# A hybrid trunk layer in float32: FFN down by the seven-product scheme, its block sums made early, stage joints rewritten

## Chip, cores and metric

The kernel runs on one core of a Trainium2 chip. The metric is the device time of one execution in microseconds (us). A figure for a kernel is the median of its runs.

## What is computed

One layer over 2048 tokens of width 1024, all in float32: an RMS norm, a mixing stage of two head groups (a gated MLP over chunks and a matrix-memory recurrence), an FFN with a causal depthwise convolution of three taps, a gate that adds an embedding `p`, and a last RMS norm. In short form (`W` stands for the weights):

```
h  = rms(x) ;  x1 = x + concat(gmlp(h W_uv), mlstm(h W_qkvo)) W_out
f  = rms(x1) W_up            # 2048 x 5632, two halves a, b of 2816
act = silu(conv3(a)) * conv3(b)
x2 = x1 + act W_down         # 2048 x 2816 times 2816 x 1024
out = rms(x2 + sigmoid(rms(x2) W_pg) * (p W_pe))
```

## The kernel before

**Numbers.** A float32 product is made of three matmuls on operands split in a rounded high part and a low rest: high by high, high by low, low by high. The split is a copy (ScalarE, or VectorE in `wsplit`) for the high part and a subtraction on VectorE for the low one (`wsplit` L102 for the mix stage, `halves` L678 and `split` L684 for the later ones).

**Mix stage (0 to 871 us).** Four blocks `b` of 512 tokens, one after the other. Each has four `tok_group`s (token-major products; L325 to L327), of which group 3 comes last, then eight `qk_tile`s and four `u_tile`s (L118 to L121), whose results pass a convolution on VectorE (`cv`, L480) and a SiLU on ScalarE (`qk`, L482); `head_a` (L490 to L492) is the first that needs a `qk`. Tiles 0 and 4 feed the first `head_a`. A block's residual goes to DRAM (`x1s`). The FFN's input of a block is made one block later by `make_h` (L640), called through `pend[1]()` at L439: for each of four `kk` it loads 512 KB of `x1s` into an `xs` buffer of `xpool`, scales it on VectorE (`ffn_in`, L204) and writes it to DRAM (`td`). In an odd block it also loads two 256 KB tiles (`hs`) and makes four block sums for the up product (L214, L216, L218, L220), each written out. `xpool` has two buffers, shared by `xs` and `hs`, so a `kk` can load only when the writes of the one before have landed.

**FFN (871 to 2218 us).** Two halves of 1024 tokens, each up and then down. Up multiplies 2x2 blocks by seven products in place of eight, with the order in `ORDER`; `build_t` loads the token operands from `td` into 28 slots `k`, and the block sums of `w_up` are made on the fly (`Up.prep`). Its results pass `Up.conv` and are written as `act`. Down (class `Down`, L819) is the plain product: per half two token blocks `th`, 22 steps `j`, 8 column tiles `d` and 3 matmuls, into four pairs of PSUM banks:

```
for d in range(KD):
    PE.matmul(ps, hi[:, c], t[:, :HALF], ...)     # L848
    PE.matmul(ps, hi[:, c], t[:, HALF:], ...)     # L849
    PE.matmul(ps, lo[:, c], t[:, :HALF], ...)     # L850
```

`load` brings 512 KB of `w_down` and 256 KB of `act` per step, `prep` splits both.

**Embedding stage (2218 to 2479 us).** `Ple.run` for four token blocks; the last one in two halves. The norm's chain `st1`, `st2`, `st3` of `SumSq` (L146 to L187) ends in a broadcast row `rB`.

**What sets the order.** In the FFN a table of steps (`Steps`): each step names the steps ahead at which its loads and splits are emitted. Everywhere the tile scheduler then orders each engine's list, and each engine, and SyncE (SP) which issues all the DMAs, runs its list strictly in that order, waiting at the first instruction that is not ready.

Of the kernel before, what the change touches and what calls it, by code (L numbers as in the profile page):

```python
# [15 lines left out]
P = 128  # L16
# [14 lines left out]
SLOTS = {"k": (28, 1024), "r": (7, 1024), "f": (4, 1024), "w": (2, 3072), "m": (8, 512), "x": (8, 512)}  # L31
# [10 lines left out]
def trunk_kernel(ctx: ExitStack, tc: tile.TileContext, xT, pT, w_u, w_qk, w_v0, w_v1,  # L42
# [33 lines left out]
    tds = [{q: dram.tile([P, 4, TB], F32, name=f"td{s}_{q}") for q in range(1, 8)} for s in range(NH)]  # L76
    acts = [[dram.tile([P, TH], F32, name=f"act{s}_{j}") for j in range(NJ)] for s in range(NH)]

    col = const.tile([P, NCOL], F32, name="col")
    DMA.dma_start(col, cols)  # L80

# [20 lines left out]
    def wsplit(src, n, eng=None, leng=None):  # L102
        st = wpool.tile([P, 1024], F32, tag="wst", name="wst")
        DMA.dma_start(st[:, :n], src)
# [27 lines left out]
    class SumSq:  # L132
# [48 lines left out]

        def st3(self):
# [39 lines left out]

    with mx:
        big = mx.enter_context(tc.tile_pool(name="mbig", bufs=1))
# [12 lines left out]
        for k0, k1 in ((0, 1), (1, 2), (2, 4), (4, 6), (6, 8)):  # L237
# [5 lines left out]
            if k0 == 0:  # L243
                w_first = wsplit(w_v0[0], 2 * GW[0], V, V)
# [54 lines left out]
        for b in range(NB):  # L299
# [347 lines left out]
    with ExitStack() as fx:  # L647
# [25 lines left out]
        def load2(src, nm):  # L673
            t = slot("x", nm)
            DMA.dma_start(t, src)
            return t
# [38 lines left out]

        def build_t(s, prod, kk):
            T[prod, kk] = halves(load2(tds[s][prod][:, kk, :], "hx"), "k", "tt")


        class Up:  # L720
# [66 lines left out]
            def post(self, prod):  # L787
# [14 lines left out]
                else:  # L802
                    f = self.conv(1, ub)
                    V.tensor_tensor(f, f, self.fa, ALU.mult)
                    DMA.dma_start(acts[self.s][self.j], f)

        def up_half(s, extra):
            for j in range(NJ):
                o = Up(s, j)
# [9 lines left out]
        n3 = [SumSq(Slots("m"), None, None, V) for b in range(NB)]  # L819

        class Down:
            def __init__(self, s, th):
                self.s, self.th, self.b, self.w, self.op = s, th, 2 * s + th, {}, {}

            def load(self, j):
                w = self.w[j] = slot("w", "wd")
                DMA.dma_start(w[:, 0:1024], w_down[j])
                DMA.dma_start(w[:, 1024:1536], acts[self.s][j][:, self.th * HALF:(self.th + 1) * HALF])

            def prep(self, j):  # L830
                w = self.w.pop(j)
                t = halves(w[:, 1024:1536], "r", "at")
                self.op[j] = split(w[:, 0:1024], "r", "wd") + (t,)

            def fetch(self):
                self.x = []
                for q in range(4):
                    x = pairs(slot("f", "xr"))
                    DMA.dma_start(x, x1s[self.b][:, 2 * q:2 * q + 2, :])
                    self.x.append(x)  # L840

            def mm(self, j):
                if j == 0:
                    self.ps = [bank2("dn") for _ in range(4)]
                hi, lo, t = self.op.pop(j)
                for d in range(KD):
                    ps, c = self.ps[d // 2][:, d % 2, :], slice(d * 128, (d + 1) * 128)
# [4 lines left out]
            def post(self):  # L852
                n = n3[self.b]
                for q in range(4):
# [3 lines left out]
                    for i in range(2):  # L858
                        n.add(x[:, i, :])
# [20 lines left out]
        class Ple:  # L880
# [27 lines left out]
            def out_tile(self, d, si, ps):  # L908
# [14 lines left out]
                if d == KD - 1:  # L923
                    f.st1()
# [168 lines left out]
```

## Time and profile before

| | |
|---|---|
| Runs shown | 2482.81 us median of 3 (2481.03 to 2486.6) |
| Profiled execution, its own time | 2480.78 us |
| Span in its profile | 2479.0 us |
| TensorE (PE) busy | 2404.0 us, 97% |
| VectorE (DVE) busy | 1697.2 us, 68% |
| ScalarE (ACT) busy | 1066.4 us, 43% |
| DMA | 324.99 MB, mean 131 GB/s |
| Mean granted TensorE clock | 0.990 of full speed |

A row of the profile names the line, the engine, the operation, the tile written and those read, and how many there were. A busy figure on PE counts overlapping matmuls, so the rate of a dense stretch is read from a window: its length over its number of matmuls. The bracket at the end of a timeline row gives the idle time of the engine ahead of the instruction, and what ended it.

### The profile page before, as it was taken

Reading aid. Unit: us, or ns where it says so; the run is one execution under the profiler, and the core shown is the slowest. Engines: PE = TensorE matmul, PEld = TensorE weight load, DVE = VectorE, ACT = ScalarE, POOL = GpSimd, SP = SyncE. Lnnn points to the kernel's source line nnn. Section 1 sums busy time; section 2 is a strip of 40 time slices with the busy share of each in tenths; the row PEclk is TensorE's granted clock in tenths of the full one; section 3 lists DMA queues with packets and bytes.
Section 4 is the critical chain, followed back from the end, with each engine's and each line's share of the span. In section 5 each row is a group of like instructions: output and inputs, shape, how many; then the busy total and the mean of one; then the engine's idle time right before and its main releaser. Section 6 shows DMA issues by size and latency. Waiting matters only on the chain.

```text
span 2479.0 us, 30740 instructions
## 1 busy us (share of the span) xinstructions
PE 2404.0 (97%) x11596; PEld 2039.9 (82%) x11596; DVE 1697.2 (68%) x2846; ACT 1066.4 (43%) x1707; POOL 53.5 (2%) x62
## 2 busy tenths in 40 slices
PE   8999999999999979999999999999999999989997
PEld 8888987988898858888888887788888888868887
DVE  7687667688656578888776343878877746354666
ACT  3453364256236355444455332444444435332223
POOL 1000000000000000000000000000000000000000
PEclk9999999999999989999999999999999999999999
DMA  6326424472542262344227474322222266550221
GB/s 200 96 69 213 153 85 135 151 241 70 175 132 86 94 238 77 112 157 157 94 91 258 140 250 136 120 77 77 86 93 77 97 212 206 184 189 13 68 69 68
DMA packets 125173, 324.99 MB, mean 131 GB/s; under 512 B 13664, under 2 KB 15840, under 8 KB 125024
## 3 DMA queue, kind: packets, MB, share of 16 engines
q1 hardware_dynamic: 125024, 323.02, 39.3%
q8 instruction: 91, 1.49, 0.2%
q14 instruction: 58, 0.48, 0.1%
HBM read 260.05 MB, written 62.91 MB: 130 GB/s over the span
## 4 chain that ended last, share of the span: by engine, by line
PE 89%; DVE 5%; DMA 3%; ACT 2%; issue 1%; POOL 1%; SPq 0%; DVEq 0%; POOLq 0%; ACTq 0%
PE ub L764 6%; PE ub L763 6%; PE ub L762 6%; PE dn L848 6%; PE dn L849 6%; PE dn L850 6%; PE ua L764 5%; PE ua L762 5%; PE ua L763 5%; PE acc L118 4%; PE acc L119 4%; PE acc L121 4%; PE bank L118 3%; PE bank L119 3%; PE bank L121 3%; PE acc L326 3%
## 5 line engine op out<-in xcount | busy, mean ns | idle before, releaser
L762 PE MATMUL ub<-tt,sw 128*128 128x512 f32 x704 | 276.1, 392 | 13.2 <-ACT tt L680 11.6
L848 PE MATMUL dn<-at,wd 128*128 128x512 f32 x704 | 274.1, 390 | 5.0 <-ACT wd L686 3.3
L763 PE MATMUL ub<-tt,sw 128*128 128x512 f32 x704 | 275.7, 392 | 1.3 <-DVE tt L681 1.3
L764 PE MATMUL ub<-tt,sw 128*128 128x512 f32 x704 | 275.4, 391 | 0.5 <-DVE sw L687 0.5
L849 PE MATMUL dn<-at,wd 128*128 128x512 f32 x704 | 273.9, 389 | 0.0
L850 PE MATMUL dn<-at,wd 128*128 128x512 f32 x704 | 272.5, 389 | 0.0
L686 ACT ACTIVATE sw<-wr 128x1024 fp32r<-128x1024 f32 x132 | 140.3, 1063 | 289.2 <-PE ua L763 257.6
L687 DVE TENSOR_TENSOR wd<-wd 128x1024 fp32r<-128x1024 f32 x88 | 107.9, 1226 | 198.4 <-ACT wd L686 195.1
L687 DVE TENSOR_TENSOR sw<-wr,sw 128x1024 fp32r<-128x1024 f32 x132 | 161.4, 1223 | 75.7 <-ACT sw L686 75.6
L762 PE MATMUL ua<-tt,sw 128*128 128x512 f32 x528 | 205.7, 390 | 0.7 <-ACT sn L768 0.7
L763 PE MATMUL ua<-tt,sw 128*128 128x512 f32 x528 | 205.5, 389 | 0.0
L764 PE MATMUL ua<-tt,sw 128*128 128x512 f32 x528 | 205.4, 389 | 0.0
L111 DVE TENSOR_TENSOR wlo<-wst,whi 128x1024 fp32r<-128x1024 f32 (+2 forms) x144 | 158.6, 1105 | 52.5 <-ACT whi L107 31.2
L326 PE MATMUL acc<-wlo,hh 128*128 128x384 f32 (+1 forms) x512 | 175.6, 343 | 7.8 <-DVE wlo L111 7.8
L325 PE MATMUL acc<-whi,hh 128*128 128x384 f32 (+1 forms) x512 | 172.6, 342 | 8.2 <-DVE whi L109 7.7
L686 ACT ACTIVATE wd<-wd 128x1024 fp32r<-128x1024 f32 x88 | 93.2, 1059 | 192.5 <-PE dn L849 187.4
L327 PE MATMUL acc<-whi,hl 128*128 128x384 f32 (+1 forms) x512 | 174.7, 341 | 0.0
L762 PEld LDWEIGHTS ub<-tt,sw 128*128 128x128 f32 x704 | 133.1, 189 | 42.6 <-ACT tt L680 12.7
L848 PEld LDWEIGHTS dn<-at,wd 128*128 128x128 f32 x704 | 132.1, 188 | 34.5 <-ACT wd L686 4.5
L763 PEld LDWEIGHTS ub<-tt,sw 128*128 128x128 f32 x704 | 133.1, 189 | 30.2 <-DVE tt L681 2.4
L764 PEld LDWEIGHTS ub<-tt,sw 128*128 128x128 f32 x704 | 133.1, 189 | 28.3 <-DVE sw L687 0.9
L850 PEld LDWEIGHTS dn<-at,wd 128*128 128x128 f32 x704 | 132.2, 188 | 27.8 <-DVE wd L687 0.2
(296 smaller groups left out, 5073.9 us busy)
## 6 DMA issues: line engine op xcount, KB each, us to landing
wd<-w_down SPq DMA_DIRECT2D x88, 512.0 KB, 3.6
wr<-w_up SPq DMA_DIRECT2D x44, 512.0 KB, 3.6
wr<-w_up SPq DMA_DIRECT2D x88, 256.0 KB, 4.4
act<-fc SPq DMA_DIRECT2D x44, 512.0 KB, 4.0
wd<-act SPq DMA_DIRECT2D x88, 256.0 KB, 3.9
wst<-w_v SPq DMA_DIRECT2D x48, 384.0 KB, 3.2
wst<-w_qk SPq DMA_DIRECT2D x32, 512.0 KB, 3.6
wst<-w_out SPq DMA_DIRECT2D x32, 512.0 KB, 3.5
```

Of the source, the lines that this page charges most:

```text
L118: PE.matmul(ps, wh, mh, start=(i == 0), stop=False)
L119: PE.matmul(ps, wh, ml, start=False, stop=False)
L326: PE.matmul(ps[t][:, :n], a_h, rl, start=False, stop=False)
L327: PE.matmul(ps[t][:, :n], a_l, rh, start=False, stop=(k == KD - 1))
L686: A.activation(hi, x, AF.Copy)
L687: V.tensor_tensor(lo, x, hi.bitcast(F32), ALU.subtract)
L762: PE.matmul(ps, hi[:, c], t[:, :HALF], start=first, stop=False, skip_group_check=on)
L763: PE.matmul(ps, hi[:, c], t[:, HALF:], start=False, stop=False, skip_group_check=on)
L764: PE.matmul(ps, lo[:, c], t[:, :HALF], start=False, stop=last, skip_group_check=on)
L848: PE.matmul(ps, hi[:, c], t[:, :HALF], start=(j == 0), stop=False)
L849: PE.matmul(ps, hi[:, c], t[:, HALF:], start=False, stop=False)
L850: PE.matmul(ps, lo[:, c], t[:, :HALF], start=False, stop=(j == NJ - 1))
```

## The change

1. **Down in seven products.** `Down` is now one object per half. Each of the seven products of `ORDER` has 11 steps `k` of 12 matmuls (L920 to L922 of the changed file). A step loads two tiles of 256 KB into one `x` slot (four slots of 1024 columns, before eight of 512), four steps ahead, and splits them two steps ahead (`halves`, L728 and L729). Products accumulate in two pairs of banks; between products ScalarE copies a pair aside (`snap`) or VectorE adds it to the residual (`give`).
2. **Block sums of `w_down`**: new `down_sums` for each of the 11 `k`, three in each of the blocks 0 to 2 and two in block 3, placed behind group 3: two loads of 512 KB into `xpool`, four subtractions or additions of 128x512 on VectorE, four writes of 256 KB to `sds`.
3. **Block sums of `act`**: `Up.sums` in each odd `j` of up: four such operations, four writes to `ads`.
4. **`make_h`** is called behind group 3 and behind `down_sums`, no longer ahead of group 3.
5. **Joints.** The first weight tile is loaded through ScalarE's DMA queue at the start. `build_t` loads two `kk` by one DMA of 512 KB. The norm of block 0 of the last stage (`st2b`, `st3`) moves into up of half 1. `out_tile` keeps gate and product in one pair of banks. The norm of the last two halves uses a shorter chain (`q1`, `q2`), and their output leaves in DMAs of two tiles, all from VectorE.

```diff
+    def down_sums(k, pair, one):
+        p, q = pair(), pair()
+        for i, t in enumerate((p, q)):
+            DMA.dma_start(t, w_down[2 * k + i].rearrange("p (i t) -> p i t", t=TB))
+        s5, s6, s7, s3 = one(), one(), one(), one()
+        V.tensor_tensor(s5, p[:, 1, :], q[:, 1, :], ALU.add)
+        V.tensor_tensor(s6, s5, p[:, 0, :], ALU.subtract)
+        V.tensor_tensor(s7, p[:, 0, :], p[:, 1, :], ALU.subtract)
+        V.tensor_tensor(s3, q[:, 0, :], s6, ALU.subtract)
+        for n, t in ((5, s5), (6, s6), (7, s7), (3, s3)):
+            DMA.dma_start(sds[n][:, k, :], t)
...
-            if b:
-                pend[1]()
             ps = tok_group(3)
             for t in range(CPB):
                 evac(osig[:, t, 128:512], ps[t][:, 0:384], t)
+            for k in range(3 * b, min(3 * b + 3, NJ // 2)):
+                down_sums(k, lambda: xpool.tile([P, 2, TB], F32, tag="xs", name="ds"), lambda: tt("dsum"))
+            if b:
+                pend[1]()
...
+                    self.act = pairs(f)
+                    if self.j % 2:
+                        self.sums()
...
+            def load(self, prod, k):
...
+                x = self.raw[prod, k] = pairs(slot("x", "sx"))
+                DMA.dma_start(x[:, 0, :], sw())
+                DMA.dma_start(x[:, 1, :], tm())
+
+            def prep(self, prod, k):
+                x = self.raw.pop((prod, k))
+                self.op[prod, k] = halves(x[:, 0, :], "r", "dw"), halves(x[:, 1, :], "r", "dt")
...
+                for d in range(4):
+                    ps, c = bank[d // 2][:, d % 2, :], slice(d * 128, (d + 1) * 128)
+                    first = k == 0 and prod in (1, 2, 5)
+                    last, on = k == NK - 1, prod in (6, 7, 3, 4)
+                    PE.matmul(ps, w[:, c], t[:, :HALF], start=first, stop=False, skip_group_check=on)
+                    PE.matmul(ps, w[:, c], t[:, HALF:], start=False, stop=False, skip_group_check=on)
+                    PE.matmul(ps, w[:, HALF + d * 128:HALF + (d + 1) * 128], t[:, :HALF], start=False, stop=last, skip_group_check=on)
...
         def down_half(s, extra):
+            o = Down(s)
+            for i, prod in enumerate(ORDER):
+                for k in range(NK):
+                    early = [(4, lambda prod=prod, k=k: o.load(prod, k)), (2, lambda prod=prod, k=k: o.prep(prod, k))]
...
+        at(3, 5, n3[0].st2b)
+        at(3, 3, n3[0].st3)
         up_half(1, ex)
...
-        n3[0].st2b()
-        n3[0].st3()
```

**VectorE in block 2, before.** The list ends `make_h` (L204 scales, L214 to L220 sum) with the low parts of the next weight tiles (L111) between its `kk`; the convolutions of tiles 0 and 4 (L480) follow. These are the third and the fourth `kk`.

```order
L214 TENSOR_TENSOR hx<-xs 128x512
L216 TENSOR_TENSOR hx<-xs,hs 128x512
L218 TENSOR_TENSOR hx<-hx,hs 128x512
L220 TENSOR_TENSOR hx<-hs,hx 128x512
L111 TENSOR_TENSOR wlo<-wst,whi 128x1024 x2
L204 SCALAR_TENSOR_TENSOR xs<-xs,col,rB 128x512 x2
L214 TENSOR_TENSOR hx<-xs 128x512
L216 TENSOR_TENSOR hx<-xs,hs 128x512
L218 TENSOR_TENSOR hx<-hx,hs 128x512
L220 TENSOR_TENSOR hx<-hs,hx 128x512
L111 TENSOR_TENSOR wlo<-wst,whi 128x1024
L480 SCALAR_TENSOR_TENSOR cv<-ub,col,cv 128x512 x6
```

The first two `kk` stood further up, ahead of group 3's last weights and behind them.

**VectorE in block 2, changed.** First the place from group 3's last copy (`osig`) to the first `kk`: the rest of the second `down_sums` and the whole third one (L256 to L259), weights of the tiles (L117, the old L111), then the first scaling (L231, the old L204).

```order
L373 TENSOR_SCALAR osig<-acc 128x384
L257 TENSOR_TENSOR dsum<-dsum,ds 128x512
L258 TENSOR_TENSOR dsum<-ds 128x512
L259 TENSOR_TENSOR dsum<-ds,dsum 128x512
L117 TENSOR_TENSOR wlo<-wst,whi 128x1024 x2
L256 TENSOR_TENSOR dsum<-ds 128x512
L257 TENSOR_TENSOR dsum<-dsum,ds 128x512
L258 TENSOR_TENSOR dsum<-ds 128x512
L259 TENSOR_TENSOR dsum<-ds,dsum 128x512
L117 TENSOR_TENSOR wlo<-wst,whi 128x1024 x2
L231 SCALAR_TENSOR_TENSOR xs<-xs,col,rB 128x512 x2
```

Then the end of the same stretch: the third and the fourth `kk` (L241 to L247 are the old L214 to L220), and the convolutions of tiles 0 and 4 (L521, the old L480).

```order
L231 SCALAR_TENSOR_TENSOR xs<-xs,col,rB 128x512 x2
L241 TENSOR_TENSOR hx<-xs 128x512
L243 TENSOR_TENSOR hx<-xs,hs 128x512
L245 TENSOR_TENSOR hx<-hx,hs 128x512
L247 TENSOR_TENSOR hx<-hs,hx 128x512
L231 SCALAR_TENSOR_TENSOR xs<-xs,col,rB 128x512 x2
L241 TENSOR_TENSOR hx<-xs 128x512
L243 TENSOR_TENSOR hx<-xs,hs 128x512
L245 TENSOR_TENSOR hx<-hx,hs 128x512
L247 TENSOR_TENSOR hx<-hs,hx 128x512
L521 SCALAR_TENSOR_TENSOR cv<-ub,col,cv 128x512 x6
```

All four `kk` now stand behind the third `down_sums`, one after the other, with one weight tile between the first and the second, and the first convolution of the block stands behind the last of them. On PE the order at this place was four tiles, 16 small matmuls of `mix` (L555), two of tile 5's matmuls, `head_a`; it is now four tiles, `mix`, 18 of tile 5's matmuls, `head_a`. In blocks 1 and 3, where `make_h` makes no sums, the convolutions stand ahead of it, or behind its last scaling with the loads begun earlier.

**SP from up to down, half 0, before.** L827 and L828 load a step of down, L675 the token operands of the next half, L839 the residual; L805 writes the last `act`.

```order
L827 DMA wd<-w_down 128x1024
L828 DMA wd<-act_3_103 128x512
L839 DMA xr<-x1s_78 128x1024 x2
L675 DMA hx<-td_7_99 128x512
L675 DMA hx<-td_3_95 128x512 x2
L805 DMA act_21_121<-fc 128x1024
L839 DMA xr<-x1s_78 128x1024
L827 DMA wd<-w_down 128x1024
L828 DMA wd<-act_4_104 128x512
```

**SP at the same place, changed.** L903 and L904 load a step of down, L858 writes `act`, L872 a block sum of `act`.

```order
L903 DMA sx<-w_down 128x512
L904 DMA sx<-act_6_121 128x512
L912 DMA xr<-x1s_82 128x2048
L858 DMA act_20_135<-fc 128x1024
L872 DMA ad_5_108<-two 128x512
L858 DMA act_21_136<-fc 128x1024
L872 DMA ad_7_110<-two 128x512
L872 DMA ad_6_109<-two 128x512
L872 DMA ad_4_107<-two 128x512
L903 DMA sx<-w_down 128x512
L904 DMA sx<-act_8_123 128x512
```

Before, the loads of four steps stand ahead of the last `act` write and the fifth right behind it. Now the first four steps are loaded ahead, and the fifth stands behind the write of the last `act` and the three last block sums made from it. From up to down in half 1 the order is the same, with one more load between.

## Rows read from the trace of the kernel before

**Rows 1.** Windows, up 0 to down 1: length, busy us, clock, DMA share, GB/s.

```profile
905.00:1311.00 406.00, 405.31 (x1787) 335.06 (x1786) 342.05 (x379) 203.33 (x281) 1.01 (x1) 1.00 0.36 124
...
1433.00:1537.00 104.00, 104.00 (x459) 85.53 (x457) 42.53 (x50) 34.01 (x44) 0.00 (x0) 1.00 0.60 203
...
1565.00:1977.00 412.00, 411.54 (x1815) 340.59 (x1815) 322.68 (x430) 184.61 (x216) 2.99 (x2) 1.00 0.25 83
...
1977.00:2218.00 241.00, 241.00 (x1064) 199.42 (x1064) 115.51 (x129) 94.78 (x117) 0.00 (x0) 1.00 0.56 187
```

**Rows 2.** What PE waited for in all: total us, times, longest us.

```profile
PE bank L184 <- DVE dg L178: 12.0, 2, 9.6
...
PE ub L762 <- ACT tt L680: 11.6, 2, 9.0
...
PE acc L326 <- DVE wlo L111: 7.8, 5, 2.7
...
PE acc L325 <- DVE whi L109: 7.7, 3, 6.7
...
PE bank L159 <- DVE sh L148: 4.3, 1, 4.3
```

**Rows 3.** Groups by line and shape: down's first matmul line of three.

```profile
L848 PE MATMUL dn<-at,wd 128*128 128x512 f32 x704 | 274.1, 390 | 5.0 <-ACT wd L686 3.3 <-ACT fhalo L782 1.7
```

**Rows 4.** DVE's timeline in block 2: start, duration, operation, idle time before.

```profile
508.64 1.41 DVE L204 SCALAR_TENSOR_TENSOR xs<-xs,col,rB 128x512 f32<-128x512 f32 x2
...
520.48 0.56 DVE L334 TENSOR_SCALAR osig<-acc 128x384 f32<-128x384 f32 x1 [0.48 <-PE acc L327]
...
520.95 1.41 DVE L204 SCALAR_TENSOR_TENSOR xs<-xs,col,rB 128x512 f32<-128x512 f32 x2
...
524.32 0.69 DVE L220 TENSOR_TENSOR hx<-hs,hx 128x512 f32<-128x512 f32 x1
...
531.12 1.41 DVE L204 SCALAR_TENSOR_TENSOR xs<-xs,col,rB 128x512 f32<-128x512 f32 x2 [3.44 <-DMA xs<-x1s]
...
536.50 4.06 DVE L480 SCALAR_TENSOR_TENSOR cv<-ub,col,cv 128x512 f32<-128x512 f32 x6
```

**Rows 5.** Windows of densest DMA: start of up 0, start of embedding stage.

```profile
871.00:905.00 34.00, 20.42 (x66) 14.61 (x66) 24.53 (x37) 20.96 (x35) 0.00 (x0) 0.80 0.84 282
...
2218.00:2231.00 13.00, 3.37 (x10) 2.26 (x10) 12.16 (x17) 7.51 (x13) 0.00 (x0) 0.62 0.98 365
```

**Rows 6.** DMA issues: tile, count, KB each, median us from issue to landing.

```profile
wd<-w_down SPq DMA_DIRECT2D x88, 512.0 KB, 3.6
...
wd<-act SPq DMA_DIRECT2D x88, 256.0 KB, 3.9
...
hx<-td SPq DMA_DIRECT2D x56, 256.0 KB, 5.4
...
xs<-x1s SPq DMA_DIRECT2D x12, 512.0 KB, 5.4
...
td<-xs SPq DMA_DIRECT2D x20, 256.0 KB, 3.6
...
hs<-td SPq DMA_DIRECT2D x8, 256.0 KB, 5.7
```

**Rows 7.** PE's timeline in block 2: group 3's second matmuls, `head_a`'s first.

```profile
510.97 0.61 PE L326 MATMUL acc<-wlo,hh 128*128 128x384 f32 x1 [2.32 <-DVE wlo L111]
511.38 0.53 PE L327 MATMUL acc<-whi,hl 128*128 128x384 f32 x1
511.70 0.53 PE L326 MATMUL acc<-wlo,hh 128*128 128x384 f32 x1
...
543.85 0.49 PE L490 MATMUL pm<-qk 128*128 128x128 f32 x2
```

**Rows 8.** DVE's timeline from up to down, half 0: up's last product `act`.

```profile
1319.45 1.22 DVE L804 TENSOR_TENSOR fc<-fc 128x1024 f32<-128x1024 f32 x1
```

**Rows 9.** PE's timeline at the same place: down's first matmul.

```profile
1311.70 0.39 PE L848 MATMUL dn<-at,wd 128*128 128x512 f32 x1
```

More of the change, by code (lines that the diff above doesn't have):

```diff
@@ L180, in st2b, with q1, q2 @@
                                 ALU.mult)
+        def q1(self):
+            mp = pmt()
+            nt = self.n // 128
+            for c in range(nt):
+                PE.matmul(mp[:, c:c + 1], self.a[:, c * 128:(c + 1) * 128], one, start=True, stop=True)
+            r = rpool.tile([P, CPB], F32, tag="nr", name="nr")[:, :nt]
+            V.tensor_scalar(r, mp[:, :nt], 1.0 / D, EPS, ALU.mult, ALU.add)
+            G.tensor_tensor(r, r, mhalf[:, :nt], ALU.pow)
+            self.r = r
+        def q2(self):
+            nt = self.n // 128
+            dg = self.t("dgf")
+            V.tensor_tensor(dg.rearrange("p (c t) -> p c t", t=128),
+                            ident.rearrange("p (o t) -> p o t", o=1).broadcast_to([P, nt, 128]),
+                            self.r.rearrange("p (c o) -> p c o", o=1).broadcast_to([P, nt, 128]), ALU.mult)
+            bp = pmt()[:, :self.n]
+            PE.matmul(bp, ones, dg, start=True, stop=True)
+            self.rB = bp
         def st3(self):
@@ L805, in post, with sums @@
                     DMA.dma_start(acts[self.s][self.j], f)
+                    self.act = pairs(f)
+                    if self.j % 2:
+                        self.sums()
+            def sums(self):
+                p, q, k = self.prev.act, self.act, self.j // 2
+                one = Twos()
+                t7, t5, t6, t4 = [one() for _ in range(4)]
+                V.tensor_tensor(t7, q[:, 1, :], p[:, 1, :], ALU.subtract)
+                V.tensor_tensor(t5, p[:, 1, :], p[:, 0, :], ALU.subtract)
+                V.tensor_tensor(t6, t7, p[:, 0, :], ALU.add)
+                V.tensor_tensor(t4, q[:, 0, :], t6, ALU.subtract)
+                for n, t in ((7, t7), (5, t5), (6, t6), (4, t4)):
+                    DMA.dma_start(ads[self.s][n][:, k, :], t)
         def up_half(s, extra):
+            o = None
             for j in range(NJ):
-                o = Up(s, j)
+                prev, o = o, Up(s, j)
+                o.prev = prev
                 for prod in ORDER:
@@ L819, in trunk_kernel @@
         n3 = [SumSq(Slots("m"), None, None, V) for b in range(NB)]
+        NK = NJ // 2
         class Down:
[L822 to L847, printed above, removed]
-                    PE.matmul(ps, hi[:, c], t[:, :HALF], start=(j == 0), stop=False)
-                    PE.matmul(ps, hi[:, c], t[:, HALF:], start=False, stop=False)
-                    PE.matmul(ps, lo[:, c], t[:, :HALF], start=False, stop=(j == NJ - 1))
@@ L852, in post, with __init__ @@
[L852 to L870 removed]
+            def __init__(self, s):
+                self.s, self.raw, self.op, self.p = s, {}, {}, {}
@@ new lines, in snap, with give @@
+            def snap(self, bank):
+                out = []
+                for q in range(2):
+                    t = pairs(slot("k", "sn"))
+                    A.activation(t, bank[q], AF.Copy)
+                    out.append(t)
+                return out
+            def give(self, fh, th, bank, plus):
+                b = 2 * self.s + th
+                n, x = n3[b], self.x[0]
+                for q in range(2):
+                    xq = x[:, 2 * q:2 * q + 2, :]
+                    V.tensor_tensor(xq, xq, bank[q], ALU.add)
+                    if plus is not None:
+                        V.tensor_tensor(xq, xq, plus[q], ALU.add)
+                    DMA.dma_start(x2s[b][:, 4 * fh + 2 * q:4 * fh + 2 * q + 2, :], xq)
+                    for i in range(2):
+                        n.add(xq[:, i, :])
```

146 lines of the change are left out of this document (93 added, 53 removed).

## Prediction

> **What bounds the kernel now.** I read the windows by stage first, since a busy share over the whole span mixes stages [rows 1]. In both halves of up and of down TensorE (PE) is busy for the whole window at full clock, while VectorE (DVE) has 342 of 406 us at most and DMA at most 0.60 of its time. So there only fewer matmuls shorten the time, as long as nothing else grows into a bound. The reader should next see what PE waited for: the rows shown add up to 43 us, nearly all of it at the joints of stages [rows 2]. A change has two ways to gain here: matmuls in down, and these joints. I forecast against the profiled execution's 2480.8 us, 2.0 us below the median of the runs, and inside their scatter.
>
> **Down, matmuls.** Before: three lines with 704 matmuls each, 2112 [rows 3]. After: 2 halves x 7 products x 11 steps x 12 = 1848, so 264 fewer. A window of down holds 459 matmuls in 104.00 us [rows 1], 226.6 ns each; the 390 ns of one [rows 3] overlap. Their shape stays 128x512. 264 x 0.2266 = **-59.8 us**, all on the path.
>
> **Down, what feeds it.** A step is now 12 x 0.2266 = 2.72 us and needs two splits: on DVE 2 x 0.69 [rows 4], about half of the step. Banks alternate, so no copy or addition between products is waited for. These I cost at nothing; PE covers them.
>
> Loads: per half 77 steps x 2 x 262 KB = 40.4 MB, 7.3 MB for the next half's operands, 8.4 MB for the residual in and out: 56 MB in 77 x 2.72 = 209 us, 268 GB/s where the window shows 203 [rows 1]. A rate of 282 held for 34 us and 365 for 13 us [rows 5], so the rate alone should do. Latency is nearer: with four `x` slots, of which operands of the next half hold one during 48 steps of half 0, a step takes at least (landing + 1.9) / 3, where 1.9 is both splits (1.4) and an issue. That reaches 2.72 us at a landing of 6.3 us; with four slots at 9.0. The loads of these tensors land in 3.6 to 5.4 us [rows 6]. I take 0, ends 0 and +28 (a landing of 8 us in the 48 steps: (9.9 / 3 - 2.72) x 48).
>
> **Block sums.** In up, 11 odd `j` per half with four operations of 0.69 [rows 4]: 30 us of DVE more per half, 342 to 372 of 406 [rows 1]. PE hides it; without that cover it would be those 30 us per half. I take +2 for both. Those of `w_down` lie beside PE in blocks 0, 1 and 3; block 2 is next.
>
> **Block 2 of the mix stage.** This is my largest term against the change. Before, the end of group 3 is where the last `osig` copy starts, 520.5 us; the last scalings of `make_h` follow at 520.95 and 531.12; the convolutions at 536.50 end at 540.6 [rows 4], and `head_a` starts at 543.85 [rows 7], 23.4 us after group 3: just in time, PE had its four tiles until then. In the new order all four `kk` stand behind the third `down_sums`, and the convolutions behind them. From the end of group 3 (0):
> - osig and the rest of the second sum: to +2.6. Its writes go out, then the third pair of loads (3.6 us for 512 KB of this tensor [rows 6]): +7.6. Third sum, four operations: +10.4.
> - That frees `xpool`; the first `kk`'s loads land 5.4 (`xs`) and 5.7 us (`hs`) after issue [rows 6]: +16.6.
> - A `kk` can load only when the write of the one before has landed: scaling 1.4 [rows 4], write 3.6, reload 5.4 [rows 6], 10.4 us. The trace bears it out: the scalings are 12.3 and 10.2 us apart [rows 4]. Three rounds: +47.8.
> - Last `kk` 1.4 + 4 x 0.69 = 4.2, convolutions 4.1, SiLU and hand-over 0.9 (my estimate): `head_a` at **+57**.
>
> PE has work to +23.4, and 16 matmuls of tile 5 more (3.6 us) that it did later before: a wait of 57 - 23.4 - 3.6 = 30 us. Gone is the old wait of 2.3 us ahead of group 3 and the slow spell behind it (0.32 us from matmul to matmul in [rows 7], 11 of them: 1.6); after a longer idle PE will start slow again (+2). Net **+28**, ends 0 (if the rounds overlap PE's tiles after all) and +36 (12.3 us per round).
>
> The Trainium skill, page "DMA: Bandwidth & Descriptors", section "Anatomy of one DMA", fits a DMA issued by GpSimd by about 2.0 us plus its bytes over 436 GB/s, 2.6 us for 256 KB and 3.2 for 512 KB. By it, as an estimate, a round would take 7.2 us and the sum come out 10 us lower. The rows for SP's transfers are longer [rows 6], and they decide.
>
> **Blocks 1 and 3.** `make_h` no longer stands ahead of group 3's weights, and no chain of sums hangs on it. The waits for `wlo` and `whi` [rows 2], less the longest one of 6.7, at the start, and the 2.3 in block 2 [rows 7], leave 6.5, in pieces at other joints: I take -5, ends -6.5 and +3 (sums in the way of the weights).
>
> **From up to down.** Four steps are loaded ahead; the fifth's loads stand on SP behind the last `act` and its three sums. Before, that `act` was ready at 1320.7, 9.0 us after down's first matmul [rows 8, 9], with splits of operands in between that are now fewer. I take +8.5 with the sums, 1 us of issues, 3.9 to 5.4 to land [rows 6], 1.4 for the splits: +15.4 against 4 x 2.72 = 10.9. So PE waits 4.5 us, twice: +9; the wait for a bank at the old joint (1.7 [rows 3]) goes. **+7.3**, ends 0 and +14.
>
> **Other joints.** Embedding stage: the norm that PE waited 9.6 us for [rows 2] is done in up of half 1; next is the first gate tile, whose operands were loaded during down: -9.6, ends -10 and -5. Tail: the shorter chain takes most of the 4.3 us for `sh` [rows 2]: -3, ends 0 and -5. End of down 0: the waits for `wd` splits, 3.3 [rows 3]: -2.5, ends -3.3 and +4. Start of up 0: same bytes in fewer DMAs, 0, ends -4 and +4 (9.0 us wait there [rows 2]). Start: the first weight issued earlier, -1 of the 6.7 [rows 2], ends -1.5 and 0. The same page, section "Issuing engines are not separate DMA queues", has it that a second issuing engine saves only the time to issue. By that rule this term would be near 0 and the sum 1 us higher; no row here tells them apart.
>
> **Sum.** -59.8 + 28 + 2 - 5 + 7.3 - 9.6 - 3 - 2.5 - 1 = -43.6; 2480.8 - 43.6 = **2437 us**.
>
> **Rivals.**
> - *Block 2 doesn't wait long.* For it: the rounds lie beside PE's tiles in the old order, and a round of half the length would leave 14 us. Against it: two buffers for `xs` and `hs`, and the rounds of the trace. With 0 to 14 us instead of 30: 2407 to 2421, say 2414.
> - *Half 0 of down waits for loads.* Landing at 8 us under 268 GB/s: +28 in 48 steps, 2465. For it: `hs` and `hx` already take 5.4 to 5.7. Against it: `wd` loads at 187 to 203 GB/s land in under 4.
> - *Slower than before: down is bound by landing throughout.* Place: SP's loads of a step, four slots. Price: at 10.5 us, 48 steps x (12.4 / 3 - 2.72) + 106 x (12.4 / 4 - 2.72) = 68 + 40, so 2545. It outweighs the gain of 43.6 from a landing of 9.0 us (3.63 us in each of the 48 steps). No transfer in the rows comes near it.
> - *DVE becomes the bound of up.* 372 of 406 us excludes it on the mean; part of the range only.
>
> **How the numbers follow.** A measurement of this kernel can tell 0.2%, 5 us, from no change. Forecast as summed 0.62 (2428 to 2448 by its small terms), no long wait in block 2 0.18, loads short in half 0 0.12, slower 0.06, and 0.02 for a sum of mishaps that ends level. Faster 0.62 + 0.18 + 0.12 = 0.92, same 0.02, slower 0.06. The range takes the second and most of the third case: 2406 to 2464.
>
> **What would show it.** Right: 1848 matmuls in down at 226 to 228 ns; in block 2 one wait of PE of some 30 us for the SiLU of tile 4 (`qk`), with DVE waiting for `xs` loads in rounds of 10 us; two waits of 2 to 7 us for down's splits at its fifth step; no wait ahead of the first gate tile. Wrong: a step of down above 2.8 us in half 0 with landings above 6 us (second rival), or a `head_a` in block 2 less than 35 us behind group 3 (first rival).

## The result, and the profile after

The changed kernel takes 2453.82 us (median of 4 runs, 2452.77 to 2459.78); the kernel before, in the same comparison, 2481.92 (4 runs, 2478.66 to 2486.6). The ratio is 0.989, with a 95% interval of 0.9868 to 0.9913: faster by 28 us, or 1.1%. In a later comparison the same two kernels gave 2451.08 and 2482.92, ratio 0.9869 (0.9856 to 0.9883). The forecast was 2437, so the direction was right, the time lies in the range (2406 to 2464), and about a third of the expected gain of 43.6 us is missing.

The profiled execution took 2453.29 us, with a span of 2451.5; the one before had a span of 2479.0. The first thing to make of two such traces is a table of stages, because gains and losses of different stages cancel in the total. A stage here runs from its first matmul to the first matmul of the next, so it holds the wait at its own end. The last column is the forecast's terms, put to the same stages.

| Stage | before | after | difference | forecast |
|---|---|---|---|---|
| start | 6.73 | 5.92 | -0.8 | -1 |
| mix, block 0 | 219.9 | 218.0 | -1.9 | 0 |
| block 1 | 214.05 | 216.3 | +2.3 | -5, with block 3 |
| block 2 | 217.8 | 246.24 | +28.4 | +28 |
| block 3 | 222.15 | 219.34 | -2.8 | see block 1 |
| up 0 | 431.0 | 439.34 | +8.3 | +2, with up 1 |
| down 0 | 245.7 | 216.56 | -29.1 | -29.6 |
| up 1 | 421.9 | 422.75 | +0.8 | see up 0 |
| down 1 | 249.2 | 226.09 | -23.1 | -35.0 |
| embedding stage to PE's end | 242.8 | 234.51 | -8.3 | -3 |
| rest | 7.7 | 6.4 | -1.2 | 0 |

Four rows of the table hold the miss: down 1 is 12 us worse than forecast, up 0 6 to 8, blocks 1 and 3 4.5; the embedding stage gives 5 back.

Here is what PE waited for in all in the changed kernel (total us, times, longest us), to be held against [rows 2]:

```profile
PE acc L495 <- ACT cv L519: 22.6, 1, 22.6
PE ub L815 <- ACT tt L728: 13.6, 2, 9.5
PE pm L531 <- ACT qk L523: 9.4, 4, 7.5
...
PE da L926 <- ACT dt L728: 7.4, 2, 4.0
...
PE da L927 <- DVE dt L729: 5.0, 1, 5.0
PE ub L815 <- ACT sn L821: 4.0, 4, 1.7
PE acc L548 <- DVE cn L549: 2.0, 1, 2.0
PE bank L211 <- DVE dg L184: 1.9, 1, 1.9
...
PE ub L815 <- DVE ub L851: 1.7, 3, 0.8
```

The first and the third line are block 2 (22.6 and 7.5). The `da` waits for `dt` from ScalarE (7.4 in two, 4.0 and 3.5) are the two joints from up to down. The single 5.0 for `dt` from VectorE lies in down 1 and was not in the forecast. The 9.0 us wait at the start of up 0 [rows 2] is still there (9.5); the 9.6 ahead of the first gate tile is gone.

The windows of the changed kernel's up 0 and of down, with the columns of [rows 1]:

```profile
905.00:1345.00 440.00, 427.36 (x1852) 349.17 (x1853) 379.53 (x444) 215.36 (x303) 1.98 (x1) 0.99 0.44 151
1362.00:1506.00 144.00, 144.00 (x633) 118.70 (x632) 91.50 (x139) 82.12 (x141) 0.00 (x0) 1.00 0.77 256
1984.00:2066.00 82.00, 72.36 (x298) 58.05 (x297) 49.84 (x70) 39.06 (x62) 0.00 (x0) 0.94 0.69 237
```

The second line is what the matmul term rested on: 633 matmuls in 144.00 us, 227.5 ns each, at 256 GB/s, with PE never idle. The third, in down 1, holds only 298 in 82 us: 298 x 0.2275 = 67.8, so 14 us of it went to waits and slow matmuls, of which the forecast knew the 4.5 us at the joint.

The fastest and the slowest of the four kinds of loads of down, from the issue of a DMA to its landing (count, KB each, median us):

```profile
sx<-sd SPq DMA_DIRECT2D x88, 256.0 KB, 4.0
...
sx<-act SPq DMA_DIRECT2D x66, 256.0 KB, 4.6
```

They land in 4.0 to 4.6 us in the median, well below the 6.3 from which half 0 would have waited.

**Block 2.** VectorE's timeline there (start, duration, operation, idle time ahead of it and its releaser), to be read beside [rows 4]:

```profile
516.76 0.55 DVE L373 TENSOR_SCALAR osig<-acc 128x384 f32<-128x384 f32 x1
...
525.61 0.69 DVE L256 TENSOR_TENSOR dsum<-ds 128x512 f32<-128x512 f32 x1 [3.66 <-DMA ds<-w_down]
...
534.73 1.41 DVE L231 SCALAR_TENSOR_TENSOR xs<-xs,col,rB 128x512 f32<-128x512 f32 x2 [1.45 <-DMA xs<-x1s]
...
545.99 1.41 DVE L231 SCALAR_TENSOR_TENSOR xs<-xs,col,rB 128x512 f32<-128x512 f32 x2 [6.05 <-DMA xs<-x1s]
...
555.43 1.42 DVE L231 SCALAR_TENSOR_TENSOR xs<-xs,col,rB 128x512 f32<-128x512 f32 x2 [5.37 <-DMA xs<-x1s]
...
565.80 1.42 DVE L231 SCALAR_TENSOR_TENSOR xs<-xs,col,rB 128x512 f32<-128x512 f32 x2 [6.31 <-DMA xs<-x1s]
...
569.79 4.06 DVE L521 SCALAR_TENSOR_TENSOR cv<-ub,col,cv 128x512 f32<-128x512 f32 x6
```

From the end of group 3 (the last `osig` copy, 516.76) the third sum, the four `kk` and the convolutions follow one another, and the rounds are 11.3, 9.4 and 10.4 us long. PE at the same place:

```profile
561.01 0.80 PE L495 MATMUL acc<-hh,whi 128*128 128x512 f32 x1 [22.59 <-ACT cv L519]
...
574.57 0.80 PE L531 MATMUL pm<-qk 128*128 128x128 f32 x2 [7.50 <-ACT qk L523]
```

`head_a` starts at 574.57, 57.8 us behind group 3, where the sum had 57. The wait comes in two parts, and the first has a releaser that the forecast did not see. ScalarE's timeline shows it:

```profile
560.18 0.78 ACT L519 ACTIVATE cv<-acc,col 128x512 f32<-128x512 f32 x1 [23.49 <-DMA td<-hx]
```

Tile 5's bank comes free by the copy `cv`, and `cv` takes its buffer from the same pool of eight as the block sums `hx`, so ScalarE sat 23.5 us until the write of a `kk`'s sums had landed. The tile's matmuls then run, and PE waits for the convolutions.

### The profile page after: what moved, and what is told of

Its sections match the earlier page's. It is cut to its first block, busy times and chain, and to the rows that moved or that the text cites. A ratio compares the mean times of both kernels' runs of the same rounds, so it can differ in the third digit from the quotient of the medians.

```text
span 2451.5 us, 31204 instructions
## 1 busy us (share of the span) xinstructions
PE 2350.1 (96%) x11336; PEld 1990.9 (81%) x11336; DVE 1815.1 (74%) x3107; ACT 1103.0 (45%) x1848; POOL 52.9 (2%) x59
## 3 DMA queue, kind: packets, MB, share of 16 engines
q8 instruction: 89, 1.46, 0.3%
## 4 chain that ended last, share of the span: by engine, by line
PE 75%; DVE 10%; DMA 8%; ACT 2%; issue 2%; POOL 1%; SPq 1%; DVEq 0%; ACTq 0%; POOLq 0%
PE ub L815 6%; PE ub L816 5%; PE ub L817 5%; PE ua L815 4%; PE ua L816 4%; PE ua L817 4%; PE acc L124 3%; PE acc L125 3%; PE acc L127 3%; PE gt L124 3%; PE gt L125 3%; PE gt L127 3%; PE acc L364 3%; PE acc L366 3%; PE acc L365 3%; PE da L927 2%
## 5 line engine op out<-in xcount | busy, mean ns | idle before, releaser
L735 DVE TENSOR_TENSOR sw<-wr,sw 128x1024 fp32r<-128x1024 f32 x132 | 161.5, 1223 | 46.5 <-ACT sw L734 44.7
L117 DVE TENSOR_TENSOR wlo<-wst,whi 128x1024 fp32r<-128x1024 f32 (+2 forms) x144 | 158.5, 1104 | 25.9 <-ACT whi L113 14.5
L729 DVE TENSOR_TENSOR dt<-sx,dt 128x512 fp32r<-128x512 f32 x154 | 106.2, 690 | 63.6 <-ACT dt L728 63.4
L926 PE MATMUL da<-dt,dw 128*128 128x512 f32 x352 | 139.7, 397 | 7.4 <-ACT dt L728 7.4
L927 PE MATMUL da<-dt,dw 128*128 128x512 f32 x352 | 140.2, 398 | 5.0 <-DVE dt L729 5.0
L928 PE MATMUL da<-dt,dw 128*128 128x512 f32 x352 | 139.6, 397 | 0.0
L729 DVE TENSOR_TENSOR dw<-sx,dw 128x512 fp32r<-128x512 f32 x154 | 106.0, 688 | 43.7 <-ACT dw L728 43.5
L728 ACT ACTIVATE dt<-sx 128x512 fp32r<-128x512 f32 x154 | 96.3, 626 | 92.6 <-PE db L928 46.0
L113 ACT ACTIVATE whi<-wst 128x1024 fp32r<-128x1024 f32 x80 | 84.1, 1057 | 104.1 <-PE acc L125 40.2
```

Of the source, the lines that this page charges most:

```text
L117: (leng or V).tensor_tensor(lo[:, :n], st[:, :n], hi[:, :n].bitcast(F32), ALU.subtract)
L729: V.tensor_tensor(t[:, HALF:], x, t[:, :HALF].bitcast(F32), ALU.subtract)
L735: V.tensor_tensor(lo, x, hi.bitcast(F32), ALU.subtract)
L927: PE.matmul(ps, w[:, c], t[:, HALF:], start=False, stop=False, skip_group_check=on)
```

## The experiments

Each is an edit of the changed kernel, and is compared with the changed kernel's profiled execution, stage by stage. Four concern block 2, two down, two up 0, and three the sum. All but the last three are one execution each. In the kernels that leave a stage alone, its length still varies: a block of the mix stage by 1.5 to 3 us, up 0 by 5.7 (436.9 to 442.6), a half of down by 3 to 4.3, the embedding stage by 0.4. Differences below these tell nothing.

### Block 2: `make_h` put back ahead of group 3

```diff
+            if b == 2:
+                pend[1]()
             ps = tok_group(3)
...
-            if b:
+            if b in (1, 3):
                 pend[1]()
```

> Block 2's make_h is put back ahead of group 3; its three down_sums stay behind group 3. Theory A (what stands ahead of the block's first convolutions is one chain of seven turns through the two xpool buffers, four kk and three sums, so it does not matter which of them are behind group 3): the kk run beside group 3, the sums follow at about 9 us each and end some 45 us behind group 3; PE still waits 20 to 25 us in block 2, against 30.7 us in the changed kernel; block 2 gets 5 to 9 us shorter, the time falls to 2445 to 2449 us. Rival B (the place of make_h alone makes the wait): the wait goes, block 2 falls from 246 to 218 us and the time to about 2426 us.

It took 2452.37 us. Block 2 fell from 246.24 to 243.34, and its waits changed so:

```profile
PE acc L497 <- ACT cv L521: 14.9, 1, 14.9
PE pm L533 <- ACT qk L525: 8.7, 4, 6.8
```

The two waits together are 21.7 us where they were 30.1, but the old wait of 2.3 for `wlo` ahead of group 3 is back, and the stage is only 2.9 shorter. So the place of `make_h` is not the main thing: with either order, seven turns through two `xpool` buffers (three `down_sums`, four `kk`) stand ahead of the convolutions. The size was missed: 2.9 us came back where 5 to 9 were expected.

### Block 2: no sums of `w_down` in this block

```diff
-            for k in range(3 * b, min(3 * b + 3, NJ // 2)):
+            for k in ((0, 1, 2, 3), (4, 5, 6, 7), (), (8, 9, 10))[b]:
```

> make_h stays behind group 3, but block 2 makes no down_sums (blocks 0 and 1 make four each, block 3 three). Theory A: without the sums' turns the kk begin during group 3 and the chain ends about when the tiles do; PE's wait in block 2 falls from 30.7 to between 0 and 8 us, and blocks 0, 1 and 3 grow by 0 to 8 us each since their own chains are one turn longer; the time is 2425 to 2440 us. Rival B (the place of make_h alone makes the wait): block 2 still waits 20 us or more.

2441.06 us. Block 2 took 219.02, 27.2 less, with `make_h` where the change puts it; of the 22.6 a wait of 2.6 is left. Nothing else was touched in the block, so the sums in front of the `kk` are what costs. But a fourth sum in block 0 cost 10.7 us there (228.7 for 218.0), more than the 0 to 8 expected, and one in block 1 2.7, which is within the spread: in block 0 too they do not come free.

### The turns spread over the block

```diff
+            def bg():
+                if units:
+                    units.pop(0)()
...
             a = head_a(0, q0, k0)
+            bg()
             mix(0, g0)
             k1, o0 = qk_tile(5, lambda f: head_b(*a, f))
+            bg()
```

(and so at seven places; each `down_sums` or `kk` is one unit)

> The seven turns (kk of make_h, sums) are no longer one batch behind group 3: one is emitted behind each of seven places from the first head_a on. Theory A: no convolution stands behind more than one turn, PE's wait in block 2 falls from 30.7 to under 5 us, block 2 from 246 to 216 to 220 us, the time to 2422 to 2428 us. Rival C (VectorE runs its list in order, so each turn that waits for its loads holds up the recurrence behind it): one to three us per turn come back, block 2 stays at 225 to 235 us.

2454.92 us. Block 2 took 238.97, above what either theory expected, and the other blocks grew by 4.4, 2.9 and 3.9. The waits moved to the tiles behind (in the whole kernel; the first line was 7.5 in four in the changed kernel):

```profile
PE acc L578 <- DVE hc L571: 19.2, 9, 7.2
PE pm L534 <- ACT qk L526: 11.0, 4, 6.7
```

VectorE's waits for `xs` and `ds` loads in this block fall from 24.3 to 8.1 us, but the turns now stand ahead of the heads' own operations on VectorE, and PE waits for those. Spreading alone is no cure.

### Block 2's three sums moved to the output product of block 3

```diff
-            for k in range(3 * b, min(3 * b + 3, NJ // 2)):
+            for k in ((0, 1, 2), (3, 4, 5), (), (6, 7))[b]:
...
             for d in range(KD):
+                if b == NB - 1 and d in {0: 8, 1: 9, 2: 10}:
+                    down_sums({0: 8, 1: 9, 2: 10}[d], lambda: xpool.tile([P, 2, TB], F32, tag="xs", name="ds"), lambda: tt("dsum"))
```

> The three down_sums of block 2 and the last one are moved to the last part of block 3 (its output product), where no further block's input is streamed through xpool; block 3 makes two behind group 3 as before. Theory A: block 2 falls from 246 to 217 to 221 us as in the kernel without sums there, blocks 0 and 1 stay at 216 to 218 us, block 3 and the joint behind it grow by 0 to 4 us; the time is 2422 to 2430 us. Rival J (the sums cost the same wherever they lie, since VectorE and DMA are short in the mix stage): block 3 grows by 10 us or more.

2425.79 us: block 2 220.07 (-26.2), block 3 220.13 (+0.8), which makes two sums behind group 3 as before and three in its output product. VectorE's timeline in block 2 shows why:

```profile
513.62 1.41 DVE L231 SCALAR_TENSOR_TENSOR xs<-xs,col,rB 128x512 f32<-128x512 f32 x2
...
527.55 1.41 DVE L231 SCALAR_TENSOR_TENSOR xs<-xs,col,rB 128x512 f32<-128x512 f32 x2 [3.22 <-DMA xs<-x1s]
...
538.57 1.42 DVE L231 SCALAR_TENSOR_TENSOR xs<-xs,col,rB 128x512 f32<-128x512 f32 x2 [5.81 <-DMA xs<-x1s]
...
543.57 0.75 DVE L521 SCALAR_TENSOR_TENSOR cv<-ub,col,cv 128x512 f32<-128x512 f32 x1
```

The rounds are as long as ever (13.9 and 11.0 us), but the first `kk` is scaled at 492.70, during the groups, and the last at 538.57 where it was 565.80. So three sums cost little in a place where no tile's convolution stands behind them: block 3 took 219.0 to 220.7 in the three kernels that have them there, 217.8 to 219.3 in those that leave it alone, 1.4 us less in the mean.

### Down 1: the loads of `w_pg` ahead of their splits

In the changed kernel ScalarE's timeline around the 5.0 us wait of down 1 shows two splits of `w_pg` (`wg`) and the next split for down:

```profile
2046.61 1.06 ACT L734 ACTIVATE wg<-wst 128x1024 fp32r<-128x1024 f32 x1 [4.50 <-DMA wst<-w_pg]
...
2058.59 1.06 ACT L734 ACTIVATE wg<-wst 128x1024 fp32r<-128x1024 f32 x1 [4.42 <-DMA wst<-w_pg]
...
2060.59 0.61 ACT L728 ACTIVATE dw<-sx 128x512 fp32r<-128x512 f32 x1
```

SP had issued the second one's load at 2052.25. The program places the split of `w_pg` right behind that load, so ScalarE waits for the landing, and the splits of down's next steps (L728) wait behind it in its list. Of the eight `w_pg` splits three wait 3.9 to 4.5 us like this, one 1.3 and the others under 1. PE pays more than its wait:

```profile
2063.90 0.80 PE L927 MATMUL da<-dt,dw 128*128 128x512 f32 x1 [5.03 <-DVE dt L729]
```

```profile
2064.00:2069.00 5.00, 5.00 (x12) 3.94 (x13) 4.06 (x7) 1.29 (x3) 0.00 (x0) 0.50 0.89 291
2070.00:2075.00 5.00, 5.00 (x24) 4.10 (x23) 1.29 (x2) 1.37 (x3) 0.00 (x0) 1.00 1.01 373
```

Behind the wait the granted clock is 0.50, the level of 1.2 GHz, and 12 matmuls take 5 us, 0.43 each; from 2070 it is 1.00 (2.4 GHz) again, with 24 in 5 us. What the matmuls start further apart than 0.2275 us (where it is over 0.30) adds up to 8.1 us here (5.2 in the wait, 2.9 behind it), and to 1.7 at two smaller stops of this half, at 2037 and 2049.

The edit issues each load four steps earlier and leaves the split where it is:

```diff
+        def pg_load(d):
+            rawg[d] = load4(w_pg[d])
+
         def pg(d):
-            wpg[d] = split4(w_pg[d], "k")
+            wpg[d] = split(rawg.pop(d), "k", "wg")

         for d in range(KD):
+            ex.setdefault(6 + 4 * d, []).append((4, lambda d=d: pg_load(d)))
             ex.setdefault(6 + 4 * d, []).append((0, lambda d=d: pg(d)))
```

> In down of half 1 the load of each w_pg tile is issued four steps ahead of its split, not right ahead of it; nothing else changes. Theory D (ScalarE runs its list in order and stands 4.4 us at each w_pg split waiting for the landing, while down's own splits stand behind it): the waits of PE for down's splits after its fifth step (1.3 and 5.9 us at two places, some 9 us in all) go, down 1 falls from 226 to 216 to 219 us, the time to 2444 to 2447 us. Rival E (these waits come from DMA being short at 240 to 290 GB/s): no change, 2452 to 2455 us.

2445.05 us; down 1 took 215.76, 10.3 less, and a window of it (columns as before) is dense again:

```profile
2006.00:2205.00 199.00, 199.00 (x880) 164.77 (x879) 132.70 (x191) 112.60 (x185) 0.00 (x0) 1.00 0.77 257
```

880 matmuls in 199 us, 226.1 ns each; the changed kernel had 836 in the same window. Bytes and work are the same in both, and DMA moves 257 GB/s now for 242 in the changed kernel: the loss was where the load stood ahead of its split, not the rate of DMA or the work on ScalarE. Both smaller stops are gone too, and 8.1 + 1.7 = 9.8 is nearly all of the 10.3.

### The joints from up to down: the last sums of `act` later

```diff
-                    if self.j % 2:
+                    if self.j % 2 and self.j < NJ - 1:
                         self.sums()
+                    last_up[self.s] = self
...
             o = Down(s)
+            extra.setdefault(6, []).append((0, lambda: last_up[s].sums()))
```

In the changed kernel SP's list at the joint of half 0 reads, and ScalarE's below it:

```profile
1352.02 0.32 SPq L858 DMA_DIRECT2D act<-fc  x1
1352.75 1.77 SPq L872 DMA_DIRECT2D ad<-two  x3
1354.61 0.40 SPq L903 DMA_DIRECT2D sx<-w_down  x1
```

```profile
1358.45 0.63 ACT L728 ACTIVATE dw<-sx 128x512 fp32r<-128x512 f32 x1 [7.99 <-DMA sx<-w_down]
```

PE stops there for the split:

```profile
1360.13 0.80 PE L926 MATMUL da<-dt,dw 128*128 128x512 f32 x1 [3.95 <-ACT dt L728]
```

Down's fifth step is loaded behind the last `act` and its sums, as forecast. The edit makes those sums at down's sixth step (they are first read by a later product).

> The block sums of the last j of up are made six steps into down instead of right behind the last act, in both halves, so the loads of down's fifth step no longer stand on SP behind three writes that wait for VectorE. Theory F (the 4.3 and 3.8 us that PE waits at down's fifth step come from this place in SP's list): both waits fall to under 1.5 us, down 0 and down 1 get 3 to 4.5 us shorter each, the time falls by 5 to 9 us to 2445 to 2449 us. Rival G (they come from VectorE's backlog of convolutions, or from the landings): the waits stay above 3 us, the time within 2 us of 2453.8.

2440.22 us. Both waits for `dt` at the joints are gone; down 0 took 211.09 (-5.5) and down 1 219.06 (-7.0). That is more than the waits of 4.0 and 3.5 and more than the 3 to 4.5 expected: in the changed kernel PE's matmuls stand 0.43 us apart for a while behind each, and that goes too. Counted as above, the joints cost 5.9 us (4.1 + 1.7) and 6.7 (3.6 + 3.1). The wait at the `w_pg` split, which this edit leaves alone, is still there (5.7 us).

### Up 0: the norm's loads ahead of their use

In the changed kernel PE waits three times for `sn` in up 0. The first wait, of 0.7 us, stood in the kernel before too; the second comes about so (ScalarE, then SP):

```profile
1008.64 0.63 ACT L147 ACTIVATE sq<-xl 128x512 f32<-128x512 f32 x1 [3.51 <-DMA xl<-x1s]
1009.18 0.58 ACT L821 ACTIVATE sn<-ub 128x512 f32<-128x512 f32 x1
```

```profile
1000.84 2.06 SPq L872 DMA_DIRECT2D ad<-two  x2
1002.95 1.33 SPq L1076 DMA_DIRECT2D xl<-x1s  x1
```

The squares for block 3's norm stand behind their own load, and that load on SP now stands behind the writes of a block sum; PE's bank copy `sn` stands behind the squares. The edit issues these loads three products earlier and `st3` a little later:

```diff
+        def last_load(k):
+            xls[k] = pairs(slot("x", "xl"))
+            DMA.dma_start(xls[k], x1s[NB - 1][:, k:k + 2, :])
...
         for k in range(KD):
+            if k % 2 == 0:
+                ex.setdefault((3 + k // 2, 2), []).append((3, lambda k=k: last_load(k)))
             at(3 + k // 2, (2, 7)[k % 2], lambda k=k: last_sum(k))
...
-        at(7, 3, nl.st3)
+        at(8, 1, nl.st3)
```

> In up of half 0 the loads of the last block's norm (xl) are issued three products ahead of the squares that read them, and the norm's last part (st3) two products later; the block sums of act stay. Theory H (up 0 lost its 8 us at squares and norm steps that wait in ScalarE's and VectorE's lists with PE's releasers behind them, not by VectorE's load as such): the waits of 2.1, 1.4 and 2.3 us at 1008, 1048 and 1068 us go, up 0 falls from 439 to 433 to 435 us. Rival I (VectorE is simply too full with the block sums): the waits move to other places and up 0 stays at 437 to 441 us.

2449.52 us; up 0 took 434.72 (-4.6), and the waits for `sn` are down from 3.4 to 0.7 us in that stage. 3.7 us of its 8.3 remain above the kernel before. The edit has two parts, the loads and `st3`, and the run doesn't tell them apart.

### Up 0: half 0's block sums of `act` on GpSimd

```diff
+                E = V if self.s else G
-                V.tensor_tensor(t7, q[:, 1, :], p[:, 1, :], ALU.subtract)
...
+                E.tensor_tensor(t7, q[:, 1, :], p[:, 1, :], ALU.subtract)
...
```

(all four operations)

> In up of half 0 the block sums of act are made by GpSimd instead of VectorE; the loads stay as in the changed kernel. Rival I (VectorE too full): with 30 us of work less on it up 0 falls from 439 to 431 to 434 us. Theory H: the waits for xl loads and the norm stay, only those at 1130, 1169 and 1208 us (0.8 to 1.2 us, for a sum on VectorE) go; up 0 falls to 435 to 438 us.

2477.1 us, and up 0 460.06: 20.7 longer, outside every expectation. VectorE's groups in up 0 (count, then busy us and mean ns of one, then idle time ahead), first of the changed kernel, then of this one:

```profile
L735 DVE TENSOR_TENSOR sw<-wr,sw 128x1024 fp32r<-128x1024 f32 x62 | 75.8, 1223 | 10.9 <-ACT sw L734 10.7
...
L831 DVE SCALAR_TENSOR_TENSOR fc<-ua,col,fc 128x1023 f32<-128x1023 f32 x21 | 26.8, 1278 | 0.0
...
L798 DVE TENSOR_TENSOR wr<-wr 128x1024 f32<-128x1024 f32 x21 | 25.6, 1220 | 0.0
```

```profile
L735 DVE TENSOR_TENSOR sw<-wr,sw 128x1024 fp32r<-128x1024 f32 x59 | 84.5, 1432 | 5.0 <-ACT sw L734 5.0
L798 DVE TENSOR_TENSOR wr<-wr 128x1024 f32<-128x1024 f32 x20 | 29.3, 1463 | 0.4
L831 DVE SCALAR_TENSOR_TENSOR fc<-ua,col,fc 128x1023 f32<-128x1023 f32 x20 | 25.6, 1281 | 2.0 <-ACT fc L828 2.0
```

And the costliest of the four on GpSimd:

```profile
L871 POOL TENSOR_TENSOR two<-fc,two 128x512 f32<-128x512 f32 x9 | 18.4, 2041 | 0.7
```

An operation that takes 0.69 us on VectorE takes 1.4 to 2.0 on GpSimd, and VectorE's two groups of subtractions shown, each of two SBUF tiles, get 17 and 20% slower in the mean. From 880 us to the stage's end the waits that the profile gives for PE grew from 21.1 to 35.2 us. Counted as above, the stage loses 39.5 us in place of 18.8, which is the whole of the 20.7: 15.4 of it in the waits, 5.3 in the slower matmuls behind them.

### The four cures together, one more load ahead, and the change again

One kernel takes the sums to block 3's output product, the `w_pg` and norm loads ahead and the last sums of `act` later; a second also loads `build_t`'s operands two steps ahead of their split; the third is the change itself.

> Four repairs in one kernel: the sums of block 2 in block 3's last part, the last block sums of act six steps into down, the w_pg loads four steps ahead, the norm's loads of up 0 three products ahead. If the causes are as shown and independent, the stages' gains add: block 2 -26, down 0 -5.5, down 1 -7 and -10.3, up 0 -4.6, block 3 +1: 2453.8 - 52 = 2402 us (2398 to 2407), 0.967 to 0.970 of before. If the repairs only move the waits to the next late transfer, the sum falls short: 2410 us or more.

> As the run before, and the 512 KB loads of half 1's token operands in down 0 are issued two steps ahead of their splits, not right ahead of them. If waits of a split for a transfer just issued are what still costs down 0 its 2 to 5 us, down 0 falls to 209.5 to 211 us, and the time by 1 to 4 us; if the four x slots run short instead, down 0 grows by up to 10 us.

> The changed kernel as it is, on the same chip as the two runs before it: 2452 to 2456 us, 0.987 to 0.990 of before.

Together: **2400.57 us** (5 runs, 2397.17 to 2403.91) beside 2482.92 before (9 runs), ratio 0.9667 (0.9654 to 0.9681). The four single gains, measured on their stages (26.2, 10.3, 12.5 and 4.6, in all 53.6), nearly add up: beside the changed kernel in the same comparison (2451.08) the four together give 50.5, 3 us less, which single executions can't tell from their sum. This version beats both kernels. Both halves of down are dense in it:

```profile
1304.00:1515.00 211.00, 209.87 (x925) 173.19 (x924) 143.16 (x213) 116.96 (x202) 0.00 (x0) 1.00 0.75 254
1937.00:2147.00 210.00, 209.08 (x923) 172.82 (x922) 140.75 (x205) 115.22 (x189) 0.00 (x0) 1.00 0.75 252
```

925 matmuls in 211 us; a half has 924, and the window's ends hold one more. What is left of its waits is led by the start of up 0:

```profile
PE ub L819 <- ACT tt L730: 12.8, 2, 9.9
```

The earlier loads of `build_t` gave 2401.74 us, ratio 0.9671 (0.9658 to 0.9684): no difference, and down 0 was 213.05 for 211.15. The 1 to 4 us that were expected did not come: those loads, right ahead of their splits, cost PE nothing that these runs can tell.

## Why the prediction was right or wrong

**Right.**
- *Down, matmuls.* Forecast 226 to 228 ns, found 227.5; with the cures each half takes 211 us, which is 924 x 0.228.
- *Down, what feeds it*, as far as loads go. Median landings of 4.0 to 4.6 us at 256 GB/s exclude "half 0 of down waits for loads" and "down is bound by landing": down 0 came out at -29.1 for -29.6.
- *Block 2 of the mix stage.* +28.4 for +28, `head_a` 57.8 us behind group 3 for 57, the rounds 10.4 in the mean for 10.4. "Block 2 doesn't wait long" is false. The forecast had one wait of 30 us for `qk`; there are two, 22.6 and 7.5, and the first ends with a buffer that `cv` shares with `hx`. So the sum was right and one releaser in it was not seen.
- *From up to down.* 4.0 us at the joint of half 0 for 4.5. The releaser, down's fifth step behind the last `act` and its sums, is as forecast, and moving the sums took the wait away. The size was not: the term priced the waits (9 for both), and with the slower matmuls behind them the joints cost 12.5, by what their removal gave back.

The rounds are also where a page was weighed. The Trainium skill, page "DMA: Bandwidth & Descriptors", section "Anatomy of one DMA", gives a fit for DMAs issued by GpSimd, by which a round came out at 7.2 us, as an estimate. These DMAs are issued by SP, and the runs show 9.4 to 11.3 here, and 13.9 and 11.0 with the sums elsewhere: the trace does not agree with the fit for them, and it decides.

**Luck.** The main case gave 2428 to 2448 by its small terms, and 2453.8 lies outside. The range reaches there only because it took in most of the case "half 0 of down waits for loads", which did not happen. So the range held by its breadth, and the terms below are what was missed.

**Wrong.**
- *Down, what feeds it: "These I cost at nothing; PE covers them."* This step failed, by some 10 of the 12 us missing in down 1; the other 2 are the slower matmuls at the joint (6.7 for 4.5). It counted the splits' busy time (half of a step) and the landing of down's own loads, and not what else stands in ScalarE's list. A step of down is 2.72 us now; three of the eight `w_pg` splits stop ScalarE for 3.9 to 4.5 us, and splits are made only two steps ahead. Issuing those loads earlier gave back 10.3 us with all else equal. The trace of before had the same wait, eight times in down 1, 2.6 to 3.0 us each, and I did not read it, since PE never waited for it: a step then was 24 matmuls, 5.4 us. Its first, on ScalarE's timeline of the kernel before:

```profile
2004.72 1.06 ACT L686 ACTIVATE wg<-wst 128x1024 fp32r<-128x1024 f32 x1 [2.59 <-DMA wst<-w_pg]
```

- *Block sums, +2.* Up 0 lost 8.3. The term weighed the 30 us of VectorE against its mean share; what hurt was again order. Counted as above, the first 50 us of the stage lose the same in both kernels (10.8), and behind them the kernel before loses nothing. The changed one loses 5.4 us at three places of block 3's norm (two waits for `sn`, one for `dg`) and 2.6 at three waits for the additions L851; that is 8.0 of the 8.3. 4.6 came back by issuing the norm's loads earlier. Ahead of L851 VectorE's list has, among the block sums of `act`, those of the last block's input (L241 to L247), and one of these waits 0.5 to 1.3 us for a load (`hl`) each time; no run tried this alone, so the cause is argued, not shown. Up 1, with the same sums and without that norm's loads, lost 0.8, so the sums' own cost is small. The rival "DVE becomes the bound of up" is not what happened: VectorE is busy 380 of 440 us.
- *Blocks 1 and 3, -5.* The waits for `wlo` in these blocks are gone (2.2 in block 1, 2.7 in block 3), but only -0.6 came. In block 1 a new wait of 2.0 us for `cn` stands in their place: VectorE waits 2.28 us for an `xs` load ahead of it. The rest of block 1's +2.3 was not followed, and it is within the spread of a block's length.
- *Other joints.* The embedding stage gained 8.3 for 3. The wait ahead of the first gate tile is gone as forecast; beyond it, this stage's first 14 matmuls stood 0.43 us apart behind that wait (granted clock 0.50 from 2229 to 2234) and now follow at 0.23, which is 3.0 us that the term, priced by the wait alone, left out. PE's waits in the stage fell by 3.7, from 8.8 to 5.1 (two at the tail, where 6.7 were); the rest was not followed. The start gained 0.8 for 1; other kernels with the same start show 6.1 to 6.7 against the 6.73 of before, so a gain between 0 and 0.8 can't be told apart.

## What to carry to other kernels

A load whose first use stands right behind it, on an engine that runs its list in order, can stop everything behind that use for a landing, however idle the engine is in the mean. And a stop of 4 to 5 us cost PE 1.7 to 3.1 us more here, in slower matmuls behind it. So cost a moved or faster stage by the list: for each load, where it is issued, where it is first read, and whose work stands behind that reader. When the steps get shorter, every such place that was covered before has to be looked at again. And work that passes through a pool of two buffers is a chain of landings, so its place should be where nothing urgent stands behind it: three sums cost 26 us in one place and 1 to 2 in another.

## What the runs showed of the hardware

GpSimd's work makes some of VectorE's slower. With sums on GpSimd, VectorE's subtraction of two 128x1024 tiles in SBUF went from 1.22 to 1.43 us in the mean (L735) and from 1.22 to 1.46 (L798); the convolution, which reads PSUM, stayed at 1.28 (L831). The Trainium skill, page "SBUF — State Buffer", section "SBUF: two separate sides", says that VectorE and GpSimd share a pair of ports that one of them holds for a whole instruction, and that a VectorE operation with two SBUF inputs is among those that meet a GpSimd one there. The trace agrees as to which operations are slowed; the one of this size that is not, VectorE's product L857 of two SBUF tiles (1.22 us in both), is the one whose end GpSimd's sums wait for. The price, 17 and 20% in the mean of these two groups, is the run's. No run shows GpSimd's operations without VectorE beside them, so whether they are slowed too is open.
